# Query factors by way of DRAM, and output tiles spread over three stages of a decoder trunk

## The chip, the cores and the metric

The kernel runs on one core of a Trainium2 chip. The metric is the device time of one execution in microseconds, as the median of several runs. Its engines are named as in the profile: PE (TensorE, with PEld for its weight loads), DVE (VectorE), ACT (ScalarE), POOL (GpSimd) and SP (SyncE, which only issues DMAs here).

## The reference, cut to what matters

One layer of a hybrid decoder, for a prompt of 2048 rows and for 8 samples of 8 rows, 1024 columns, all in float32:

```
x  = x + concat([ha, cb]) @ w_out                  # mLSTM and convolution, output projection
hc = rmsnorm(x, norm_x)
sc = (hc @ x_wq) . mem_k  * M**-0.5                # 4 heads, 256 memory tokens
x  = x + (softmax(sc) . mem_v) @ x_wo              # mem_k, mem_v = rmsnorm(mem) @ x_wk, x_wv
x  = x + (gelu(conv3(fa)) * fg) @ f_wdown          # ConvFFN; y = rmsnorm(x)
```

For the prompt the weights are folded into the memory: since the scores are linear in `hc`, `x_wq . mem_k` is computed once (the key fold) and multiplied with the rows; since the output is linear in the probabilities, `mem_v . x_wo` is computed once too (the value fold). The sample rows have their own memory for each of the 8 samples and are attended without folds (`sample_attention`).

## The kernel before, in words

**Arithmetic.** Every large product is made of three matmuls on float32 numbers split into a high and a low part (`mm3`, L152; `split`, L294: a cast on ACT for the high part, a subtraction on DVE or POOL for the low). The products with the folded weights go by a scheme of seven block products in place of eight; `right_factors` (L1077) turns four blocks of the folded weight into seven factors, `seven_products` uses them, `left_sums` makes the seven left factors of a pair of row tiles.

**Order.** The program names all work in one order; a planner then sets each engine's own order by simulated readiness, with earlier work of the program first. Tiles that share a tag take turns in its buffers, and are given them in the order of the program: tag "xt" of the pool `xtp` has six of 512 KB. Eight PSUM banks are shared too, by turns: banks D and F hold the halves of output tiles, A, G, D and E those of the folds, B and C (and E and F in the key fold) transposes.

**Stages around the change.**

- *Tail* (to about 770 us): end of the mLSTM, convolution tails, and the first eight output tiles. An output tile (`out_part`, L1193) is one of 16 row tiles of 128 rows (a 17th holds the 64 sample rows): `out_load` (L1183) fetches the concatenated rows `craw` and splits them (`ct`), and fetches the rows of x; two halves of 24 matmuls each against `w_out`, one PSUM bank each, are added to x, and the tile is stored to `x1_d`. `TAIL_OUT` says how many are done by here.
- *Memory stage* (`memory_kv`, L1002): 256 memory rows are fetched, normalised and transposed to `hm`, and multiplied with x_wk and x_wv in four halves of 48 matmuls. It is a generator that yields eight times, twice in each half; an output tile follows each second yield.
- *Value fold* (`fold_values`, L1145): `transposed` (L1031) fetches V back from DRAM (`mv`), transposes and splits it to `mT`; the products with x_wo give blocks, and `right_factors` seven factors, stored to DRAM (`mo_d`). It yields ten times; the remaining output tiles lie between. K is transposed here too (`mk`).
- *Key fold* (`fold_keys`, L1091): rows of x_wq are transposed and split (`rows_t`) into the tile `pair`, multiplied with K, scaled, and made into the seven query factors. `put` splits each of the 28 blocks straight into `wf`, which stays in SBUF.
- *Scores* (`scores`, eight pairs of row tiles): `pair_in` (L1399) fetches two row tiles and normalises them, `pair_factors` (L1377) transposes them (banks B, C; copies `a`), sums them on POOL and splits the seven left factors `l`. Seven products, softmax, store.
- *Output rows* (`out_rows`): the value factors are fetched (14 DMAs of 512 KB, tile `raw`, tag "xt") and split into `wf` again; eight pairs of probabilities are handled like the rows before, with the steps of `sample_attention` between, from pair `SIDE_FROM` on, four steps to a pair. After them the ConvFFN begins.

Of the kernel before, what the change touches and what calls it, by code (L numbers as in the profile page):

```python
# [9 lines left out]
F32 = mybir.dt.float32  # L10
# [9 lines left out]
P = 128  # L20
D = 1024
KT = D // P
# [8 lines left out]
N_RAW = 6  # L31

CONV_BLOCKS = [(0, 1, 12), (1, 2, 12), (3, 2, 12), (5, 2, 12), (7, 1, 12)]
TAIL_OUT = 8
MLSTM_STEPS = 2, 1, 1
W2_EARLY = 4
H2_BUFS = 10
# [3 lines left out]
KV_POOL = 2  # L41
OUT_POOL = 10
TAIL_LAG = 8
FV_STEPS = 3
KT_COPY = lambda nc: [nc.vector.tensor_copy] * 2
B_ENG = 2
MO_ENG = lambda nc: [nc.vector, nc.gpsimd, nc.vector, nc.gpsimd]
L_BUFS = 2, 6
FB_BUFS = 6
ROWS_AHEAD = 2  # L50
ROWS_AT = 0
FV_RAW = 4
FV_WT = 6
FT_BUFS = 4
KT_BUFS = 3
SIDE_FROM = 1
NORM_V = 2
L_POOL = ()
A_BUFS = 9
# [36 lines left out]
def trunk_kernel(ctx: ExitStack, tc: tile.TileContext, i: dict, o: list):  # L96
    nc = tc.nc
    V, A, G, T, SY = nc.vector, nc.scalar, nc.gpsimd, nc.tensor, nc.sync
# [8 lines left out]
    def dram(name, shape):  # L107
        return dr.tile(shape, F32, name=name, tag=name)
# [55 lines left out]
    xtp = xw = ctx.enter_context(tc.tile_pool(name="xw", bufs=6, side="right", reuse_waits="tile"))  # L164
# [5 lines left out]
    def banks(*tags):  # L170

        turn = cycle(tags)

        def get():
            tag = next(turn)
            return ps.tile([P, 512], F32, name="ps" + tag, tag=tag, bufs=PS_BANKS[tag])

        return get
# [115 lines left out]
    def split(hi, lo, src, gain=None, eng=None):  # L294
        if gain is None:
            A.copy(hi, src)  # L296
            tt(lo, src, f(hi), ALU.subtract, eng)
        else:
            act(hi, src, AF.Copy, scale=gain)
            stt(lo, src, gain, f(hi), ALU.mult, ALU.subtract)  # L300
# [701 lines left out]
    def memory_kv():  # L1002

        with tc.tile_pool(name="kva", bufs=1, side="right", reuse_waits="tile") as kva:
            xts = []
            for j in range(2):
                t = xtp.tile([P, D], F32, name="xt", tag="xt")
                SY.dma_start(t, i["mem_prompt"][0, j * P:(j + 1) * P, :])
                xts.append((t, P))
            hm = kva.tile([P, 2, KT, M], F32R, name="hm")  # L1010
            norm_x(xts, hm.rearrange("p z k n -> p (z k n)")[:, :D], V)
            make_h(xts, "g_mem", hm, mmps, True)
            for key, out, scr in (("x_wk", memk_p, mk_d), ("x_wv", memv_p, mv_d)):
                for half in range(2):
                    hs = slice(half * 512, half * 512 + 512)
                    pts = [mmps() for _ in range(2)]
                    for k in range(KT):
                        if k % 4 == 0:
                            yield
                        w = load_w(kva, i[key][0][k * P:(k + 1) * P, hs], 512, 3, raws=(kva, 4),  # L1020
                                   eng=G if k % KV_POOL == KV_POOL - 1 else V)[0]
                        for j in range(2):
                            c = slice(j * P, j * P + P)
                            mm3(pts[j], (hm[:, 0, k, c], hm[:, 1, k, c]), (w[:, 0], w[:, 1]), k == 0, k == KT - 1)
                    for j in range(2):
                        t = kva.tile([P, 512], F32, name="kvo", tag="kvo", bufs=2)
                        A.copy(t, pts[j])
                        SY.dma_start(out[0, 0, j * P:(j + 1) * P].rearrange("m h d -> m (h d)")[:, hs], t)
                        SY.dma_start(scr[j][:, hs], t)
# [61 lines left out]
    def fold_keys(pools, mT, ps_, tps_):  # L1091

        def load(j):
            if j < KT:
                raws.append(row_tile(i["x_wq"][0][order[j] * P:(order[j] + 1) * P, :]))

        def rows_t(j):
            load(j + ROWS_AHEAD)
            raw = raws[j]
            wT = pools[j % 2].tile([P, 2, D], F32R, name="pair", tag="pair")  # L1100
            for half in range(2):
                pt = tps_()
                hs = slice(half * 512, half * 512 + 512)
                for k in range(4):
                    transpose(pt[:, k * P:(k + 1) * P], raw[:, half * 512 + k * P:half * 512 + (k + 1) * P])
                split(wT[:, 0, hs], wT[:, 1, hs], pt)
            return wT

        def tmp():
            return pools[1].tile([P, 512], F32, name="ft", tag="ft", bufs=FT_BUFS)  # L1110

        order = [r + z for r in range(KT // 2) for z in (0, KT // 2)]
        raws = []
        for j in range(ROWS_AHEAD):
            load(j)
        yield
        nxt = rows_t(0)
        dst = yield

        def put(q, k, x, eng=None):  # L1120
            split(dst[q][:, 0, k], dst[q][:, 1, k], x, eng=eng)

        bs = []
        for j, r in enumerate(order):
            wT, nxt = nxt, rows_t(j + 1) if j + 1 < KT else None
            for half in range(2):
                pt = ps_()
                for z in range(2):
                    for kt in range(2):
                        k = 4 * half + 2 * z + kt  # L1130
                        c = slice(k * P, k * P + P)
                        mm3(pt[:, z * M:(z + 1) * M], (wT[:, 0, c], wT[:, 1, c]),
                            (mT[:, 0, k], mT[:, 1, k]), kt == 0, kt == 1)
                b = pools[1].tile([P, 512], F32, name="b", tag="b", bufs=FB_BUFS)
                if half < B_ENG:
                    ts(b, pt, col("g_x", r), ALU.mult)
                else:
                    act(b, pt, AF.Copy, scale=col("g_x", r))
                bs.append(b)
            if j % 2:  # L1140
                right_factors(put, r % 4, *bs, tmp, G)
                bs = []
            yield
# [49 lines left out]
    def out_part(t, loaded=None):  # L1193
        nt = P if t < NT else S
        ct, xt = loaded or out_load(t)
        for half in range(2):
            pt = mmps()
            gemm_tm(pt, ct, 0, nt, wout, half)
            hs = slice(half * 512, half * 512 + 512)
            tt(xt[:nt, hs], xt[:nt, hs], pt[:nt], ALU.add)  # L1200
        SY.dma_start(x1_d[t], xt[:nt])

    side = sample_mlstm()
# [84 lines left out]
    outs = list(range(NT))  # L1288
# [64 lines left out]

    tps, smps = banks("B", "C"), banks("E")
    SC = M ** -0.5
    mo_d = [dram(f"mo{q}", [P, KT // 2, 512]) for q in range(7)]
    p_d = [dram(f"p{t}", [P, D]) for t in range(NT)]

    def softmax(pt, p, nt, scale, nscale, w=2):
# [221 lines left out]
    fms = ExitStack()  # L1581
    fm = fms.enter_context(tc.tile_pool(name="fm", bufs=1, reuse_waits="tile"))
    pps = banks("A", "A", "G", "D", "E")
    for j, _ in enumerate(memory_kv()):
        if j % 2:
            out_part(outs.pop(0))
    out_part(NT)
    with tc.tile_pool(name="fv", bufs=1, reuse_waits="tile") as fv:
        out_part(outs.pop(0))
        fold = fold_values(fv, transposed(fv, mv_d, tps), pps,  # L1590
                           lambda: fv.tile([P, 512], F32, name="ft", tag="ft", bufs=FT_BUFS))
        for _ in range(FV_STEPS):
            next(fold, None)
        mT = transposed(fm, mk_d, tps)
        pairs = [fm]
        keys = fold_keys(pairs, mT, pps, banks("E", "F"))
        for j, _ in enumerate(fold):
            if outs:
                out_part(outs.pop(0))
            if j == ROWS_AT:  # L1600
                next(keys)
        while outs:
            out_part(outs.pop(0))
    next(keys)
    wos.close()
    wa2.close()
    wfs = ExitStack()
    wfp = wfs.enter_context(tc.tile_pool(name="wfp", bufs=1, side="right", reuse_waits="tile"))
    fks = ExitStack()
    pairs.append(fks.enter_context(tc.tile_pool(name="fk", bufs=1, side="right", reuse_waits="tile")))  # L1610

    def factors():
        return [wfp.tile([P, 2, KT // 2, 512], F32R, name=f"wf{q}", tag=f"wf{q}") for q in range(7)]

    wf = factors()
    keys.send(wf)
    for _ in keys:
        pass
    xs0 = pair_in(0)
    fms.close()  # L1620
    fks.close()
    aps = ExitStack()
    ap = aps.enter_context(tc.tile_pool(name="ap", bufs=1, reuse_waits="tile"))
    l_turn = cycle([(pa, L_BUFS[0])] * L_BUFS[0] + [(ap, L_BUFS[1])] * L_BUFS[1])
# [5 lines left out]
    pps = banks("A", "A", "G", "D", "F", "E")  # L1630
    nxt = pair_factors(xs0)
    with tc.tile_pool(name="scp", bufs=1, reuse_waits="tile") as scp:
        for p in range(NT // 2):
            left, nxt = nxt, pair_factors(pair_in(p + 1)) if p + 1 < NT // 2 else probs_in(0)
            scores(scp, p, left)
    mo = factors()
    for q in range(7):
        for k in range(0, KT // 2, 2):
            raw = xtp.tile([P, 2, 512], F32, name="raw", tag="xt")
            SY.dma_start(raw, mo_d[q][:, k:k + 2])  # L1640
            for z in range(2):
                split(mo[q][:, 0, k + z], mo[q][:, 1, k + z], raw[:, z], eng=MO_ENG(nc)[k + z])
    pps = banks("A", "A", "G", "D", "F")
    with tc.tile_pool(name="pp", bufs=1, reuse_waits="tile") as pp:
        side = sample_attention(pp)
# [288 lines left out]
```

## Time and profile before

| | us |
|---|---|
| three runs: median (lowest to highest) | 2969.03 (2966.44 to 2973.68) |
| the profiled execution, its own time | 2968.27 |
| its span, first to last instruction | 2966.6 |
| mean granted TensorE clock | 0.972 of full |
| TensorE busy | 2807.9 (95%) |
| DVE, ACT, POOL busy | 2142.2 (72%), 1534.5 (52%), 1109.8 (37%) |

The stages named above stand in the trace at about: tail to 771, memory stage to 875, value fold to 967, key fold to 1024, scores to 1195, output rows to 1450, ConvFFN to the end. A busy engine counts as busy at whatever clock it was granted, so for TensorE the granted clock is read beside its busy time: 1.00 is its upper level, 2.4 GHz, and a matmul takes twice as long at the lower.

### The profile page before, as it was taken

To read this page: it belongs to the slowest core of one execution; us is meant where nothing else is said; L and a number is where in the kernel's file an instruction comes from. 1 tells how busy PE (TensorE), PEld (TensorE's weight loads), DVE (VectorE), ACT (ScalarE), POOL (GpSimd) and SP (SyncE) were. 2 spreads that over 40 slices of the span, in tenths; PEclk is the share of its full clock that TensorE was granted. 3 is DMA by queue.
4 is the path that set the end of the run, shared out by engine and by line. 5 is a ranking of instruction groups with operands and counts; after the bars stand their busy time and mean duration, and the time that the engine had idled before them with its cause. 6 is when DMAs were issued, how large, how long until landed. Compare 5 with 4: busy or idle time off the path is not lost.

```text
span 2966.6 us, 49315 instructions
## 1 busy us (share of the span) xinstructions
PE 2807.9 (95%) x17924; PEld 2479.4 (84%) x17924; DVE 2142.2 (72%) x3937; ACT 1534.5 (52%) x3134; POOL 1109.8 (37%) x1299
## 2 busy tenths in 40 slices
PE   7999989999799799899899999999999999999998
PEld 6889889976678688676588988999989999899987
DVE  4588898873123888744598889878797767877776
ACT  4667678871232765412464446655466545544433
POOL 1558565451120632633433325333253222522222
PEclk9999999997899999999899999999999999999999
DMA  7644433244456423656745555655465545644432
GB/s 185 194 139 160 124 97 117 90 161 152 165 184 222 141 82 109 212 193 240 266 162 169 166 171 195 189 160 160 144 219 160 158 135 162 187 131 133 131 116 76
DMA packets 336939, 471.80 MB, mean 159 GB/s; under 512 B 33421, under 2 KB 238707, under 8 KB 336688
## 3 DMA queue, kind: packets, MB, share of 16 engines
q1 hardware_dynamic: 336696, 468.66, 49.2%
q8 instruction: 141, 2.31, 0.3%
q14 instruction: 102, 0.84, 0.1%
HBM read 361.68 MB, written 107.26 MB: 158 GB/s over the span
## 4 chain that ended last, share of the span: by engine, by line
PE 72%; DVE 14%; DMA 6%; issue 4%; ACT 2%; POOL 1%; SPq 1%; DVEq 0%; POOLq 0%; ACTq 0%
PE psA L150 21%; PE psD L150 14%; PE psF L150 14%; PE psE L150 9%; PE psG L150 9%; DVE psG L124 2%; DMA raw<-in_f_wup 2%; DVE wt L127 2%; PE psC L147 1%; PE psB L147 1%; DVE raw L127 1%; DVE acc L124 1%; DVE u L127 1%; DVE wf L127 1%; DMA xt<-x 1%
## 5 line engine op out<-in xcount | busy, mean ns | idle before, releaser
L296 ACT CAST wt<-raw 128x512 fp32r<-128x512 f32 x872 | 528.8, 620 | 529.2 <-PE psA L150 150.6
L127 DVE TENSOR_TENSOR wt<-raw,wt 128x512 fp32r<-128x512 f32 x660 | 512.2, 792 | 123.5 <-ACT wt L296 119.7
L127 POOL TENSOR_TENSOR wt<-raw,wt 128x512 fp32r<-128x512 f32 x212 | 306.5, 1449 | 703.9 <-ACT wt L296 572.2
L150 PE MATMUL psA<-R,wt 128*128 128x256 f32 (+1 forms) x2448 | 334.1, 287 | 4.1 <-DVE R L124 1.6
L150 PEld LDWEIGHTS psA<-R,wt 128*128 128x128 f32 x2448 | 313.8, 190 | 7.7 <-DVE R L124 1.8
L127 POOL TENSOR_TENSOR cside<-cside,cprod 128x512 f32<-128x512 f32 (+2 forms) x248 | 250.9, 1012 | 123.1 <-ACT cprod L119 90.0
L124 DVE SCALAR_TENSOR_TENSOR psG<-ue,vc,psG 128x512 f32<-128x512 f32 (+2 forms) x448 | 256.9, 573 | 22.8 <-ACT psG L119 16.0
L150 PE MATMUL psA<-wt,ht 128*128 128x512 f32 (+1 forms) x768 | 191.0, 395 | 0.0
L150 PE MATMUL psD<-R,wt 128*128 128x256 f32 (+1 forms) x1248 | 178.5, 288 | 6.7 <-DVE R L127 2.8
L150 PE MATMUL psF<-R,wt 128*128 128x256 f32 (+1 forms) x1248 | 179.3, 288 | 4.4 <-DVE R L124 1.7
L150 PE MATMUL psE<-R,wt 128*128 128x256 f32 (+1 forms) x1224 | 174.3, 287 | 5.8 <-DVE R L127 3.0
L150 PE MATMUL psG<-R,wt 128*128 128x256 f32 (+1 forms) x1224 | 175.3, 288 | 1.9 <-DVE R L124 1.3
L150 PEld LDWEIGHTS psD<-R,wt 128*128 128x128 f32 x1248 | 163.7, 191 | 10.4 <-DVE R L127 3.8
L150 PEld LDWEIGHTS psA<-wt,ht 128*128 128x128 f32 (+1 forms) x768 | 140.6, 185 | 34.9 <-DVE u L127 0.2
L150 PEld LDWEIGHTS psF<-R,wt 128*128 128x128 f32 x1248 | 163.4, 190 | 6.2 <-DVE u L127 2.6
L150 PEld LDWEIGHTS psE<-R,wt 128*128 128x128 f32 x1224 | 159.4, 190 | 9.6 <-DVE R L127 4.3
L150 PEld LDWEIGHTS psG<-R,wt 128*128 128x128 f32 x1224 | 160.3, 191 | 3.1 <-DVE R L124 1.6
L119 ACT ACTIVATE cprod<-ue,vc 128x512 f32<-128x512 f32 (+2 forms) x248 | 146.8, 605 | 28.4 <-POOL cside L127 22.0
L150 PE MATMUL psA<-wf,l 128*128 128x512 f32 x516 | 132.2, 404 | 10.8 <-DVE u L127 5.8
L124 DVE SCALAR_TENSOR_TENSOR y<-fe,vc,y 128x512 f32<-128x512 f32 x176 | 130.5, 778 | 14.4 <-ACT y L119 14.4
L127 POOL TENSOR_TENSOR y<-y,u 128x256 f32<-128x256 f32 x110 | 97.8, 898 | 107.0 <-DVE u L127 89.5
L150 PEld LDWEIGHTS psA<-wf,l 128*128 128x128 f32 x516 | 97.8, 193 | 38.7 <-issue 13.2
(608 smaller groups left out, 6096.1 us busy)
## 6 DMA issues: line engine op xcount, KB each, us to landing
raw<-sum SPq DMA_DIRECT2D x132, 512.0 KB
raw<-in_f_wup SPq DMA_DIRECT2D x110, 512.0 KB
raw<-in_f_wdown SPq DMA_DIRECT2D x88, 512.0 KB
xt<-x SPq DMA_DIRECT2D x48, 512.0 KB
sum<-raw SPq DMA_DIRECT2D x44, 512.0 KB
raw<-in_f_wup SPq DMA_DIRECT2D x66, 256.0 KB
xt<-in_x_prompt SPq DMA_DIRECT2D x32, 512.0 KB
x<-xt SPq DMA_DIRECT2D x32, 512.0 KB
```

The costliest lines, as they stand in the source:

```text
L119: A.activation(out, in_, func, bias=bias, scale=scale)
L124: V.scalar_tensor_tensor(out=out, in0=in0, scalar=s, in1=in1, op0=op0, op1=op1)
L127: (eng or V).tensor_tensor(out=out, in0=a, in1=b, op=op)
L147: T.transpose(out, in_, ident[:n, :n])
L150: T.matmul(out, lhsT, rhs, start=start, stop=stop)
L296: A.copy(hi, src)
```

## The change

Output tiles: six instead of eight are done in the tail. One is loaded ahead of the memory stage and its matmuls are called after the memory stage's first step. Of the other nine, two come between the K/V products, four in the value fold and three in the key fold. The sample's tile (`NT`) stays behind the K/V products.

Query factors: the key fold's `put` stores the 28 blocks to DRAM (`wf_d`, 256 KB each) instead of splitting them; behind the key fold `load_factors` fetches them by 14 DMAs of 512 KB into the tag "xt" and splits them into `wf`, ahead of the first pair's rows. The value factors go through the same function, as before. The key fold's second pool now lies on the left side, where the value fold's was.

Sample attention: its steps lie between the products from pair 0 on instead of pair 1.

```
-TAIL_OUT = 8
+TAIL_OUT = 6
-FV_STEPS = 3
-ROWS_AT = 0
-SIDE_FROM = 1
+SIDE_FROM = 0
@@ fold_keys
         for j in range(ROWS_AHEAD):
             load(j)
-        yield
         nxt = rows_t(0)
-        dst = yield
         def put(q, k, x, eng=None):
-            split(dst[q][:, 0, k], dst[q][:, 1, k], x, eng=eng)
+            SY.dma_start(wf_d[q][:, k], x)
@@ memory stage and folds
-    for j, _ in enumerate(memory_kv()):
-        if j % 2:
+    def next_out(at):
+        if at and outs:
             out_part(outs.pop(0))
+    t = outs.pop(0)
+    loaded = out_load(t)
+    kv = memory_kv()
+    next(kv)
+    out_part(t, loaded)
+    for j, _ in enumerate(kv):
+        next_out(j % 3 == 1)
     out_part(NT)
     with tc.tile_pool(name="fv", bufs=1, reuse_waits="tile") as fv:
-        out_part(outs.pop(0))
         fold = fold_values(fv, transposed(fv, mv_d, tps), pps, ...
-        for _ in range(FV_STEPS):
-            next(fold, None)
         mT = transposed(fm, mk_d, tps)
-        pairs = [fm]
-        keys = fold_keys(pairs, mT, pps, banks("E", "F"))
         for j, _ in enumerate(fold):
-            if outs:
-                out_part(outs.pop(0))
-            if j == ROWS_AT:
-                next(keys)
-        while outs:
-            out_part(outs.pop(0))
-    next(keys)
+            next_out(j % 3 == 0)
+    with tc.tile_pool(name="fk", bufs=1, reuse_waits="tile") as fk:
+        for j, _ in enumerate(fold_keys([fm, fk], mT, pps, banks("E", "F"))):
+            next_out(j % 2 == 0)
+    while outs:
+        out_part(outs.pop(0))
@@ factors
-    wf = factors()
-    keys.send(wf)
-    for _ in keys:
-        pass
+    def load_factors(src):
+        out = factors()
+        for q in range(7):
+            for k in range(0, KT // 2, 2):
+                raw = xtp.tile([P, 2, 512], F32, name="raw", tag="xt")
+                SY.dma_start(raw, src[q][:, k:k + 2])
+                for z in range(2):
+                    split(out[q][:, 0, k + z], out[q][:, 1, k + z], raw[:, z], eng=MO_ENG(nc)[k + z])
+        return out
+    wf = load_factors(wf_d)
     xs0 = pair_in(0)
...
-    mo = factors()
-    for q in range(7):
-...
+    mo = load_factors(mo_d)
```

## Rows read from the trace of the kernel before

**Rows 1.** the page, part 1: busy us (share) xinstructions.

```profile
PE 2807.9 (95%) x17924; PEld 2479.4 (84%) x17924; DVE 2142.2 (72%) x3937; ACT 1534.5 (52%) x3134; POOL 1109.8 (37%) x1299
```

**Rows 2.** stretches: PE, PEld, DVE, ACT, POOL busy us; PEclk, DMA, GB/s.

```profile
745.80:790.90 45.10, 29.84 (x138) 22.87 (x137) 10.25 (x21) 12.35 (x20) 9.02 (x5) 0.80 0.47 167
...
874.70:966.60 91.90, 91.59 (x420) 73.34 (x421) 33.54 (x49) 25.68 (x44) 0.00 (x0) 1.00 0.66 226
966.60:1023.70 57.10, 40.12 (x286) 37.32 (x286) 48.35 (x63) 41.10 (x74) 35.51 (x36) 0.91 0.51 166
1023.70:1050.50 26.80, 22.18 (x94) 17.33 (x93) 25.86 (x28) 16.58 (x30) 17.72 (x15) 0.94 0.09 30
...
1195.50:1250.00 54.50, 43.62 (x193) 35.20 (x193) 37.59 (x57) 26.01 (x60) 31.69 (x29) 0.91 0.66 212
```

**Rows 3.** timeline of the DMA-issue queue: start us, us, what is issued.

```profile
771.85 0.36 SPq L1008 DMA_DIRECT2D xt<-in_mem_prompt  x1
...
842.82 0.33 SPq L1190 DMA_DIRECT2D xt<-in_x_prompt  x1
...
877.70 1.72 SPq L1036 DMA_DIRECT2D xt<-mv  x2
...
889.98 0.33 SPq L1036 DMA_DIRECT2D xt<-mk  x1
```

**Rows 4.** timeline of PE in the value fold: start us, us, tile.

```profile
909.02 4.55 PE L150 MATMUL psF<-wt,ct 128*128 128x512 f32 x19
...
919.97 0.61 PE L150 MATMUL psD<-wt,mT 128*128 128x512 f32 x2
...
928.57 2.89 PE L150 MATMUL psD<-wt,ct 128*128 128x512 f32 x12
```

**Rows 5.** timeline of PE, from the tail into the memory stage.

```profile
781.88 0.48 PE L147 MATMUL psD<-ident,xt 128*128 128x128 f32 x1 [10.72 <-ACT xt L119]
...
790.91 4.21 PE L150 MATMUL psD<-wt,hm 128*128 128x512 f32 x9 [0.66 <-DVE hm L124]
...
805.40 5.75 PE L150 MATMUL psD<-wt,ct 128*128 128x512 f32 x24 [0.22 <-ACT kvo L1027]
810.99 5.60 PE L150 MATMUL psF<-wt,ct 128*128 128x512 f32 x24
```

**Rows 6.** the table of stretches, for the start of the ConvFFN.

```profile
1447.70:1475.00 27.30, 15.65 (x64) 12.12 (x62) 24.71 (x37) 16.83 (x36) 15.08 (x16) 0.64 0.98 332
```

**Rows 7.** tile wf: duration ns min/median/max, first and last start us, forms.

```profile
L296 ACT CAST wf<-raw x28: 612/622/630, 1179.4 to 1212.0; 128x512 fp32r<-128x512 f32 x28
...
L127 DVE TENSOR_TENSOR wf<-raw,wf x14: 678/1190/1782, 1180.1 to 1216.3; 128x512 fp32r<-128x512 f32 x14
L127 POOL TENSOR_TENSOR wf<-raw,wf x14: 1292/1696/1742, 1180.6 to 1213.3; 128x512 fp32r<-128x512 f32 x14
```

**Rows 8.** tiles xt and a, in the same form.

```profile
L121 ACT ACTIVATE junk<-xt x35: 1042/1057/1068, 983.4 to 2526.8; 128x1024 bf16<-128x1024 f32 x33, 32x1024 bf16<-32x1024 f32 x2
...
L296 ACT CAST l<-a x112: 602/619/666, 993.9 to 1417.3; 128x512 fp32r<-128x512 f32 x112
L127 DVE TENSOR_TENSOR l<-a,l x112: 670/686/1803, 996.8 to 1419.6; 128x512 fp32r<-128x512 f32 x112
L127 POOL TENSOR_TENSOR a<-a x64: 1267/1296/1808, 1000.6 to 1413.9; 128x512 f32<-128x512 f32 x64
L1386 ACT COPY a<-psB x32: 567/586/603, 992.4 to 1409.3; 128x512 f32<-128x512 f32 x32
```

**Rows 9.** timelines of PE and GpSimd, ends of the output rows.

```profile
1201.35 5.34 PE L150 MATMUL psA<-wf,l 128*128 128x512 f32 x12 [5.83 <-DVE u L127]
...
1237.03 7.34 PE L150 MATMUL psA<-wf,l 128*128 128x512 f32 x24 [4.00 <-ACT l L296]
...
1452.39 0.69 PE L147 MATMUL psB<-ident,xt 128*128 128x128 f32 x2 [4.08 <-ACT b L119]
...
1436.13 1.27 POOL L127 TENSOR_TENSOR xt<-xt,u 128x512 f32<-128x512 f32 x1 [12.21 <-DMA xt<-x]
```

More of the change, by code (lines that the diff above doesn't have):

```diff
@@ L1355, in trunk_kernel @@
     SC = M ** -0.5
-    mo_d = [dram(f"mo{q}", [P, KT // 2, 512]) for q in range(7)]
+    mo_d, wf_d = [[dram(f"{x}{q}", [P, KT // 2, 512]) for q in range(7)] for x in ("mo", "wfd")]
     p_d = [dram(f"p{t}", [P, D]) for t in range(NT)]
@@ L1608, in trunk_kernel @@
     wfp = wfs.enter_context(tc.tile_pool(name="wfp", bufs=1, side="right", reuse_waits="tile"))
-    fks = ExitStack()
-    pairs.append(fks.enter_context(tc.tile_pool(name="fk", bufs=1, side="right", reuse_waits="tile")))
     def factors():
         return [wfp.tile([P, 2, KT // 2, 512], F32R, name=f"wf{q}", tag=f"wf{q}") for q in range(7)]
-    wf = factors()
-    keys.send(wf)
-    for _ in keys:
-        pass
+    def load_factors(src):
[8 more added lines that the diff above has]
+    wf = load_factors(wf_d)
     xs0 = pair_in(0)
     fms.close()
-    fks.close()
     aps = ExitStack()
@@ L1635, in trunk_kernel @@
             scores(scp, p, left)
-    mo = factors()
-    for q in range(7):
[L1638 to L1642, printed above, removed]
+    mo = load_factors(mo_d)
     pps = banks("A", "A", "G", "D", "F")
```

## The prediction

> **What bounds the kernel now.** I read the page first: TensorE (PE) is busy for 95% of the span [rows 1], so time can come only from stretches in which it is idle or granted less than full clock. Then a table of stretches around the change [rows 2]. The reader is to see that the value fold (874.7 to 966.6) has no idle left (91.59 of 91.90 us at clock 1.00), while the key fold (966.6 to 1023.7) has 17.0 us idle at clock 0.91 with VectorE (DVE) busy 48 of 57, the first score pair 4.6 us, the step from tail to memory stage 15.3 us at clock 0.80, and the first output rows 10.9 us. The change moves output tiles from the full stretches to the key fold. Last, timelines, for the order in which buffers are given out, since that decides what the new reload waits for.
>
> **A rule of this kernel that the trace shows.** Buffers of one tag are handed out in program order, even when a later user is ready first. SBUF: after the load at 842.82 no load into the six "xt" buffers is issued until 877.70 [rows 3], although output tiles ended in between (at 839 and 863, going by the sequence of tiles of 11 us) and gave two buffers back, and the mk rows had long been written; mv is ahead in the program, and its last block is only then in DRAM. mk follows at 889.98. PSUM: the output tile's half in bank F runs at 909.02, its half in bank D only at 928.57, after the fold's own use of D at 919.97 [rows 4], though the operands are the same. I let this rule decide the new order.
>
> **The change part by part.** An output tile is 48 matmuls. A half of 24 starts 5.59 us after the other [rows 5], so a tile is 11.0 us wherever PE is the limit. No arithmetic is added; every term below is idle time gained or lost.
>
> *Tail and memory stage: +3, and +1.* Two tiles (22 us) leave the tail. One is loaded ahead and called behind the memory rows' transposes. The old gap: the memory rows' load is issued at 771.85 [rows 3], PE stands still for 10.72 us up to the first transpose at 781.88, the first product is at 790.91, and this runs 9 matmuls in 4.2 us, half speed [rows 5]. The forwarded tile cannot fill the gap: the eight transposes use banks D and F and come first in the program, and so the tile starts where the products started. Its two loads go ahead of the memory rows' (1 MB, some 3 us at 332 GB/s [rows 6]). The half-speed stretch is then the tile's instead of the product's. I take +3. Ends: -8, if the tail's last small work slips between the matmuls of its last tile and the rows are fetched earlier, and +6, two loads later and the norm's small steps behind the tile's split. Two of the four halves of the K/V products now follow one another directly, so that bank D is waited for: +1 (0 to 2).
>
> *Value fold: +3.* The cover between the last K/V product and the first fold product is now one tile (the sample's, 11 us), where there were three and a half. The reload of mv is issued about 3 us after that product (877.70 against 874.7); load, transposes and splits took 33 us behind other tiles, but their own steps sum to some 9 (estimate: 4 for the load, as for the memory rows, and 5 for transposes and splits). So 12 against a cover of 11; +3 for the loads of weights beside it. Ends 0 and +8. Afterwards four tiles (44 us) cover the fold as before.
>
> *Key fold: -21.* Three tiles (33 us) come in, and 28 splits (ScalarE cast and DVE or GpSimd subtraction) go to a later place. With all idle covered, the stretch takes 33 us and the old work, 40.1 us busy at clock 0.91, that is 36.5 at full: 69.5 in place of 57.1 + 33 = 90.1. DVE has 48.4 us now, less 16 subtractions; it is no limit in 69. So -21. What could spoil it: bank F is shared by row transposes and tiles in program order, and so the rows wait behind each tile; the other end is -8. The added 28 DMA stores (256 KB each, 7.3 MB) pass the same queue as the row loads: over 69 us that is 106 GB/s beside the 166 of before, below the 332 that rows 6 show.
>
> *Reload of the query factors: +25.* It takes the place of the direct splits. There are 14 loads of 512 KB, each with two casts and two subtractions, in the order factor by factor, k pairs within. The second load already reads the last k row, which is stored only at the end of the key fold. By the rule, it holds back the other twelve, and behind these pair 0's two row loads, which stood ahead of everything before. Count from the last key matmul: the first wait ends at about 2 us (a store, by the mv reload, takes about as long); the other loads are 11 x 0.524 MB and then one row tile, 6.3 MB at 332 GB/s [rows 6] = 19 us, with 2 to land: pair 0's first row is there at about 24. GpSimd keeps pace: 14 subtractions of 1.70 = 24 us [rows 7]. Then square 1.06, two small steps, scale, transpose, copy 0.59, cast 0.62, subtraction 0.69 [rows 8], with the hops some 6 to 7 us: the first product at 31. The third product needs the sum chain, four GpSimd additions of 1.30 [rows 8], a cast and a subtraction after the second row tile: about 38 to 39. Five products of 12 matmuls follow, 2.7 us each: the pair ends at about 52. Before, from 1023.7 to 1050.5, it was 26.8 [rows 2]. So +25. Low end: factors and rows stream without the wait, which leaves +3. High end: the pace of the other reload, whose 28 casts went from 1179.4 to 1212.0 [rows 7], with the last subtraction at 1216: 37 us to the rows in place of 24, so +38.
>
> For the transfers alone a page would say less. Rows 6 have 332 GB/s at a DMA share of 0.98. The Trainium skill, "DMA: Bandwidth & Descriptors", section "Anatomy of one DMA — SWDGE (gpsimd) path", fits about 2 us plus the bytes at 436 GB/s, for another issuing engine; 6.3 MB would then be 16.4 us instead of 21, and this sum some 5 us lower. I keep the measured rate.
>
> The 28 splits are neither saved nor added; only their engines change, from 16 DVE and 12 GpSimd to 14 and 14.
>
> *Sample attention from pair 0: -6.* At the start of the output rows PE waits 5.83 and 4.00 us, and at the end of the stage 4.08 [rows 9]. The side work starts and ends a pair earlier. It may fill some of the first two, and lets the rows of the next stage be normalised before the last pair ends. Against it: its nine loads go ahead of pair 1's rows in the buffer queue. GpSimd then stands as it does now at the end (12.21 us for a row load [rows 9]) and holds pair 2's sums. In between PE is full, so nothing is to be had there. I take -6, of the 14 that could go; ends -12 and +6.
>
> **Sum.** 3 + 1 + 3 - 21 + 25 - 6 = +5. The profiled execution took 2968.27 us (span 2966.6 and 1.7 around it), 0.8 below the median of 2969.03. 2968.3 + 5 = 2973. No difference is what a measurement calls anything within 0.3%, 9 us: 2960 to 2978.
>
> **Rivals.**
> - *The reload hides (faster).* If pair 0's rows are fetched ahead of the held-back factors and the factors arrive as they are stored, the reload costs +3: 2951. For it: first pairs' rows were fetched during the key fold until now, and factor B11 is complete some 4 us before the last key matmul. Against it: mk behind mv in rows 3.
> - *The reload goes at the pace of the other one (slower).* Reload +38, side work 0 because its loads meet those of the second reload: 3 + 1 + 3 - 21 + 38 + 0 = +24, 2992. It decides from the point where more than 35 us pass between last key matmul and first score product. For it: rows 7. Against it: there the buffers of the old factors had to come free as well, here they are free.
> - *The tiles don't mesh with the key rows.* Bank F makes rows and tiles alternate: key fold -8 instead of -21, with all else as forecast: +18, 2986. For it: rows 4, a half held for 19 us by the order of one bank. Against: each tile is called with one row already transposed, so that PE has its products.
>
> **Chances.** Forecast 0.36, reload hidden 0.29, slow reload 0.23, no meshing 0.12. The likeliest gives 2973, with its own range 2962 to 2982; the tails of the forecast fall about evenly to both sides. Faster 0.30, within 0.3% 0.35, slower 0.35. The range takes in the first rival and most of the other two: 2948 to 2995.
>
> **What would show it.** In the profile after: the loads of the raw factors, all but the first, issued behind the last key matmul, and pair 0's row loads behind them; PE idle for some 25 to 30 us there, then half clock; the key-fold stretch at clock 1.00 and some 70 us long with three tiles in it; the forwarded tile starting only after the last memory transpose; the first wait of the output rows shorter. I am wrong where the row loads are issued before the last raw factors, where key rows wait in ScalarE's casts while bank F holds a tile, or where other stretches (tail up to 745, the scores after pair 1, the ConvFFN after 1475) move by more than 3 us, since I hold them unchanged.

## The result and the profile after

The changed kernel takes 2990.02 us (median of 7 runs, 2977.93 to 2995.07), the kernel before 2968.28 (7 runs, 2962.64 to 2973.68): a ratio of 1.0073, 95% interval 1.0053 to 1.0094. It is slower, inside the range (2948 to 2995), and outside the forecast's own range of 2962 to 2982; the price is that of the rival "slow reload" (2992).

The page of the changed kernel, span and part 1, beside [rows 1]:

```profile
span 2993.4 us, 49433 instructions
...
PE 2814.6 (94%) x17924; PEld 2488.5 (83%) x17924; DVE 2137.2 (71%) x3935; ACT 1537.2 (51%) x3134; POOL 1102.2 (37%) x1301
```

Busy TensorE time is nearly the same; the span is 26.8 us longer. Not all of that belongs to the change. Up to the same product in the tail (its start is called the tail's point: 727.63 before, 735.22 after) every engine has the same instructions, 4810 matmuls among them. The table of stretches, of the kernel before and then of the changed one (columns as in [rows 2]):

```profile
0.00:727.63 727.63, 663.46 (x4810) 613.47 (x4810) 531.45 (x1141) 473.64 (x1164) 362.22 (x483) 0.96 0.46 140
```

```profile
0.00:735.22 735.22, 669.83 (x4810) 619.70 (x4810) 530.60 (x1141) 474.15 (x1164) 362.15 (x483) 0.95 0.45 139
```

The same instructions took 7.6 us more in the profiled execution of the changed kernel, with the granted clock at 0.95 in place of 0.96. So all further times are counted from points that both programs have:

| from ... to ... | before, us | after, us | after - before |
|---|---|---|---|
| the tail's point (727.63; 735.22) to the last key matmul (1023.80; 1006.41) | 296.2 | 271.2 | -25.0 |
| to the first output product (1201.35; 1222.99) | 177.6 | 216.6 | +39.0 |
| to the first twelve matmuls in a row into bank G in the ConvFFN (1494.70; 1519.58) | 293.4 | 296.6 | +3.2 |
| to the end of the span | 1471.9 | 1473.8 | +1.9 |

Two of these points stand in no row so far, the last key matmuls and the twelve into bank G of the kernel before:

```profile
1022.44 1.36 PE L150 MATMUL psA<-mT,pair 128*128 128x256 f32 x10
...
1494.70 1.58 PE L150 MATMUL psG<-R,wt 128*128 128x256 f32 x12
```

The changed part is the first three lines, +17.3, where the forecast had +5. The stretches of the changed kernel that answer to [rows 2]: from tail to memory stage, start of the value fold, value fold, key fold, reload, first pair:

```profile
756.60:777.30 20.70, 4.73 (x17) 2.34 (x16) 5.44 (x12) 11.43 (x19) 6.66 (x4) 0.58 0.86 307
...
859.40:874.10 14.70, 12.10 (x56) 7.27 (x56) 1.84 (x3) 1.54 (x4) 0.00 (x0) 1.00 0.89 315
874.10:942.70 68.60, 68.47 (x313) 56.50 (x314) 35.94 (x51) 26.25 (x43) 2.41 (x1) 1.00 0.79 281
942.70:1006.40 63.70, 63.52 (x401) 56.74 (x399) 32.58 (x47) 12.41 (x20) 10.35 (x8) 1.00 0.58 200
1006.40:1038.10 31.70, 0.03 (x2) 0.03 (x1) 19.98 (x17) 18.24 (x32) 23.30 (x17) 0.55 0.96 343
1038.10:1071.20 33.10, 28.48 (x117) 22.70 (x118) 16.64 (x26) 26.79 (x47) 18.06 (x25) 0.82 0.29 91
```

The key fold runs at clock 1.00 with 63.52 of 63.70 us busy. In the 31.7 us behind it (1006.40 to 1038.10) PE does nothing and the clock is at 0.55; in the next stretch it is at 0.82, so part of the first pair too runs at the lower level of 1.2 GHz.

Why PE is idle there is seen in three timelines. SP's queue (start, us, what is issued):

```profile
862.11 1.78 SPq L1034 DMA_DIRECT2D xt<-mv  x2
863.94 0.90 SPq L1034 DMA_DIRECT2D xt<-mk  x2
...
981.54 0.38 SPq L1616 DMA_DIRECT2D raw<-wfd  x1
...
1005.21 0.32 SPq L1616 DMA_DIRECT2D raw<-wfd  x1
...
1006.20 0.38 SPq L1616 DMA_DIRECT2D raw<-wfd  x1
...
1015.70 10.92 SPq L1616 DMA_DIRECT2D raw<-wfd  x6
1027.97 23.09 SPq L1400 DMA_DIRECT2D xt<-x  x10
```

The second factor load goes out at 1005.21, 24 us after the first; the other twelve follow; pair 0's row loads come only behind them, at 1027.97 (ten loads in a row, the next pairs' among them). At 862.11 and 863.94 stand mv and mk, which were 12 us apart in [rows 3]. PE then, from the last key matmuls on:

```profile
1003.61 2.80 PE L148 MATMUL psA<-mT,pair 128*128 128x256 f32 x22
1038.08 1.12 PE L145 MATMUL psB<-ident,xt 128*128 128x128 f32 x4 [31.67 <-DVE xt L129]
...
1041.42 1.22 PE L148 MATMUL psA<-wf,l 128*128 128x512 f32 x2 [0.44 <-ACT l L294]
...
1054.80 1.22 PE L148 MATMUL psG<-wf,l 128*128 128x512 f32 x2 [4.08 <-ACT l L294]
...
1071.20 0.60 PE L145 MATMUL psB<-ident,xt 128*128 128x128 f32 x4
```

PE waits 31.67 us for the first row; the first product starts at 1041.42, the third at 1054.80. GpSimd's and ScalarE's timelines say what the row waited for:

```profile
1019.99 16.34 POOL L125 TENSOR_TENSOR wf<-raw,wf 128x512 fp32r<-128x512 f32 x10 [0.66 <-ACT wf L294]
1036.41 0.19 POOL L131 TENSOR_SCALAR v<-ss 128x1 f32<-128x1 f32 x1
1036.68 0.55 POOL L141 TENSOR_TENSOR r<-v,nhalf 128x1 f32<-128x1 f32 x1
```

```profile
1032.68 1.06 ACT L119 ACTIVATE junk<-xt 128x1024 bf16<-128x1024 f32 x1 [0.15 <-DMA xt<-x]
1033.64 0.18 ACT L119 ACTIVATION_READ_ACCUMULATOR junk<-xt 128x1 f32 x1
```

The row's square is summed by 1033.8, but the two small steps to its inverse root stand behind ten subtractions of the reload, which end at 1036.3.

### The profile page after: what moved, and what is told of

The parts are those of the page before. It is cut to its first block, busy times and chain, and to the rows that moved or that the text cites. A ratio compares the mean times of both kernels' runs of the same rounds, so it can differ in the third digit from the quotient of the medians.

```text
span 2993.4 us, 49433 instructions
## 1 busy us (share of the span) xinstructions
PE 2814.6 (94%) x17924; PEld 2488.5 (83%) x17924; DVE 2137.2 (71%) x3935; ACT 1537.2 (51%) x3134; POOL 1102.2 (37%) x1301
## 4 chain that ended last, share of the span: by engine, by line
PE 74%; DVE 11%; DMA 8%; issue 3%; ACT 2%; POOL 1%; SPq 1%; DVEq 0%; POOLq 0%; ACTq 0%
PE psA L148 22%; PE psD L148 15%; PE psF L148 15%; PE psE L148 10%; PE psG L148 9%; DMA raw<-in_f_wup 2%; DVE wt L125 2%; DVE psG L122 2%; PE psB L145 1%; PE psC L145 1%; DVE raw L125 1%; DVE acc L122 1%; DMA h<-h 1%; DVE u L125 1%; DMA xt<-x 1%
```

## The experiments

Ratios are to the kernel before, with their 95% intervals; the changed kernel has 1.0073. The stretch from the last key matmul to the first output product, 177.6 us before and 216.6 after, is called the reload stretch.

**The detour alone.** To the kernel before, the stores and the reload are added; tiles and sample attention stay.

```
-            split(dst[q][:, 0, k], dst[q][:, 1, k], x, eng=eng)
+            SY.dma_start(wf_d[q][:, k], x)
...
+    for q in range(7):
+        for k in range(0, KT // 2, 2):
+            raw = xtp.tile([P, 2, 512], F32, name="raw", tag="xt")
+            SY.dma_start(raw, wf_d[q][:, k:k + 2])
...
     xs0 = pair_in(0)
```

> The kernel before with one part of the change: the key fold stores its factors to DRAM, and they are fetched and split ahead of the first pair's rows; output tiles and sample attention stay as before. Theory that the parts add up: the reload costs the 38 us that it costs in the changed kernel, and the key fold without the 28 splits gets some 10 of its 17 idle us back: 2968 + 28 = 2996. Rival, that the reload is dear only because the spread tiles keep the key fold and its transfers late: half of the price, 2978.

Measured 1.0058 (1.0039 to 1.0076). The key fold and the reload in its table of stretches:

```profile
965.29:1003.20 37.91, 32.40 (x253) 31.13 (x251) 28.82 (x45) 11.31 (x20) 9.35 (x8) 0.95 0.81 278
1003.20:1038.00 34.80, 0.00 (x0) 0.00 (x0) 22.56 (x18) 18.25 (x32) 24.28 (x18) 0.54 0.94 311
```

From its first product (965.29) the key fold takes 37.9 us without any tile in it, 5.5 of them idle, where [rows 2] has 57.1 and 17.0; 32 transposes of the first two pairs' rows, which [rows 2] has in that stretch, now lie behind it. The reload stretch is 217.1, as in the changed kernel. So both large terms come from the detour: its key fold ends 21.4 us earlier (274.7 us from the tail's point in place of 296.2), and its reload costs 39.6. The expected sum of parts was 11 too high, since the fold gained 21 and not 10.

**Two tiles back in the tail.**

```
-TAIL_OUT = 6
+TAIL_OUT = 8
```

> The changed kernel with TAIL_OUT back at 8: two tiles return to the tail, and one is left in the key fold in place of three. By the prediction's reason for the key fold's -21 (tiles cover its idle time) two thirds of that are lost: 2986 + 14 = 3000, less 3 for the step to the memory stage. Rival: it was the 28 splits that made the key fold idle. With the splits gone and no tile in it, its stretch took 36.6 us with 5.5 idle in the run wfd_only, where it had 57.1 with 17.0 idle before; then two tiles less cost at most 4: 2986 to 2990.

Measured 1.0082 (1.0068 to 1.0096), 2.7 us above the changed kernel by the ratios, and their intervals overlap. Tiles in the key fold are worth a few us, not two thirds of 21. The rival holds.

**Sample attention from pair 1 again.**

```
-SIDE_FROM = 0
+SIDE_FROM = 1
```

> The changed kernel with SIDE_FROM back at 1: the sample attention's steps lie between the products from pair 1 on. By the prediction's term (-6 for starting at pair 0) this run is 6 slower than the changed kernel: 1.0073 x 2964.6 = 2986, so 2992. Rival, from the traces: the wait at the first output product is 5.83 before and 5.82 after, and the ConvFFN's first steady product is no nearer to the start of the output rows; then starting a pair earlier is worth nothing: 2986.

Measured 1.0058 (1.0043 to 1.0073): 4 us below the changed kernel, less than the two intervals can part, and not 6 above. From first output product to the ConvFFN's bank G it is 293.0 us (1217.91 to 1510.86), with 293.4 before and 296.6 in the changed kernel. Over all thirteen profiles of this document this stretch is 292.0 to 296.6 in the seven kernels that start at pair 0 and 290.7 to 293.4 in the six that start at pair 1. The changed kernel's lines:

```profile
1222.99 5.18 PE L148 MATMUL psA<-wf,l 128*128 128x512 f32 x12 [5.82 <-DVE u L125]
...
1455.06 0.74 PE L148 MATMUL psA<-wf,l 128*128 128x512 f32 x2 [3.28 <-ACT l L294]
...
1471.74 0.44 PE L145 MATMUL psB<-ident,xt 128*128 128x128 f32 x2 [1.08 <-ACT b L117]
...
1476.79 2.93 PE L148 MATMUL psA<-R,wt 128*128 128x256 f32 x12 [2.66 <-DVE R L125]
...
1519.58 1.58 PE L148 MATMUL psG<-R,wt 128*128 128x256 f32 x12
```

The first wait is 5.82, as in [rows 9]. The 4.00 us there and the 4.08 at the end of the stage are gone or smaller (1.08), but 3.28 has come in at the last pair and 2.66 in the ConvFFN's first products. Starting a pair earlier moved waits and saved none. This kernel also differs from the detour alone only by the spread of the tiles (and, with it, the place of the key fold's pool and of its first row loads). Both have 1.0058, with intervals of about 5 us to each side. From the tail's point to the end of the span its profile is 6.3 us shorter (2251.9 and 2258.2), 4.1 of them up to the last key matmul.

**Pair 0's rows ahead of the factors.**

```
-    wf = load_factors(wf_d)
     xs0 = pair_in(0)
+    wf = load_factors(wf_d)
```

> The changed kernel with one edit: pair 0's two rows are fetched and normalised in the program ahead of the reload of the query factors. In the changed kernel 64.8 us pass from the last key matmul (1006.4) to the end of pair 0's products (1071.2), where the kernel before took 26.8. Order theory: most of that is pair 0's rows standing behind fourteen factor loads, and their normalisation behind GpSimd's subtractions; with the rows ahead, the transposes run beside the key fold, the first score product comes within 15 us of the last key matmul in place of 35, the products follow the factors as they come, and the pair ends some 40 us after the last key matmul; less some 5 us for pair 1's rows, which are then late: 2990 - 20 = 2970. Volume theory: 7.3 MB and 28 splits after the last key matmul are the price in whatever order; only the four small steps of the rows are saved, 4 us: 2986.

Measured 1.0009 (0.9998 to 1.002), 19 us below the changed kernel. SP's queue and PE:

```profile
973.63 0.38 SPq L1400 DMA_DIRECT2D xt<-x  x1
...
975.33 0.32 SPq L1400 DMA_DIRECT2D xt<-x  x1
...
979.65 0.32 SPq L1616 DMA_DIRECT2D raw<-wfd  x1
...
998.08 0.79 SPq L1616 DMA_DIRECT2D raw<-wfd  x2
```

```profile
1001.66 1.88 PE L148 MATMUL psA<-wf,l 128*128 128x512 f32 x7
...
1020.74 1.22 PE L148 MATMUL psG<-wf,l 128*128 128x512 f32 x2 [7.15 <-ACT l L294]
...
1043.37 1.12 PE L145 MATMUL psB<-ident,xt 128*128 128x128 f32 x4 [5.35 <-ACT a L1382]
```

GpSimd's and ScalarE's timelines, for what these two waits end with:

```profile
996.42 5.59 POOL L125 TENSOR_TENSOR a<-a 128x512 f32<-128x512 f32 x4
...
1016.48 3.69 ACT L294 CAST wf<-raw 128x512 fp32r<-128x512 f32 x6 [1.41 <-DMA raw<-wfd]
1020.07 2.70 ACT L294 CAST l<-a 128x512 fp32r<-128x512 f32 x5
...
1042.75 0.56 ACT L1382 COPY a<-psB 128x512 f32<-128x512 f32 x1
```

The rows are fetched at 973.63 and 975.33, and the first score product follows the last key matmul (1001.82) at once. The reload stretch is 198.5 in place of 216.6. What is left: 7.15 us for the third product and 5.35 for pair 1's second row. The third product's four sums end on GpSimd at 1002.0, but ScalarE casts them only from 1020.07 on, behind twelve casts of the reload (1009.69 to 1020.2) that wait for their loads; and the transposes of the second row wait until ScalarE has copied the first row out of bank B, at 1042.75, behind squares and scalings of later rows. So it is ScalarE's order that holds both, not GpSimd. The order theory is right; the volume is the same and the price half: 20.9 us over the 177.6 of the kernel before, where it was 39.0.

**The k pairs outside.**

```
-        for q in range(7):
-            for k in range(0, KT // 2, 2):
+        for q, k in order:
...
-    wf = load_factors(wf_d)
+    wf = load_factors(wf_d, [(q, k) for k in (0, 2) for q in range(7)])
```

> The changed kernel with one edit: the factors are fetched with the pairs of k rows outside and the seven factors inside, so that the first seven loads read what the key fold has stored 20 us before its end. Order theory: the second load, which reads the last k row, held back the other twelve; now six loads (as many as there are buffers) are issued ahead of the last key matmul, some 3 MB or 9 us less lie behind it, and pair 0's rows come 9 to 12 us earlier: 2980. Volume theory: the loads were held by the buffers or by the place of the factors, not by the last k row: no difference, 2990.

Measured 1.0046 (1.003 to 1.0063), 8 us below the changed kernel, by intervals that overlap; the reload stretch is 209.1 us in place of 216.6. Loads two to seven are issued before the last key matmul (999.58); of SP's queue the second load, the sixth and seventh, and the rows:

```profile
971.83 0.32 SPq L1615 DMA_DIRECT2D raw<-wfd  x1
...
989.36 1.14 SPq L1615 DMA_DIRECT2D raw<-wfd  x2
...
1014.06 25.72 SPq L1400 DMA_DIRECT2D xt<-x  x10
```

Ten row loads begin 14.5 us behind the last key matmul (1014.06), where it was 21.6. So the last k row did hold the other loads back, for 7 us of the 9 to 12 expected.

**GpSimd taken out of the reload.**

```
-                    split(out[q][:, 0, k + z], out[q][:, 1, k + z], raw[:, z], eng=MO_ENG(nc)[k + z])
+                    split(out[q][:, 0, k + z], out[q][:, 1, k + z], raw[:, z], eng=engs[k + z])
...
-    wf = load_factors(wf_d)
+    wf = load_factors(wf_d, [V] * 4)
```

> The changed kernel with one edit: all 28 subtractions of the reload of the query factors go to VectorE, none to GpSimd. In the changed kernel GpSimd's last subtraction ends at 1036.3 and the first row's inverse root waits for it, although the row's sum of squares was there at 1033.8. If GpSimd's pace sets the start of the scores, first transposes come 3 to 4 us earlier: 2985 to 2987. If the transfers set it, no difference: 2990 (VectorE then has 28 x 0.69 = 19 us of work in the 26 us of the loads).

Measured 1.0063 (1.0047 to 1.008), 3 us below, which the intervals alone would not part. The mechanism shows in GpSimd's and DVE's timelines:

```profile
1034.54 0.19 POOL L131 TENSOR_SCALAR v<-ss 128x1 f32<-128x1 f32 x1 [18.90 <-ACT junk L119]
...
1026.27 7.70 DVE L125 TENSOR_TENSOR wf<-raw,wf 128x512 fp32r<-128x512 f32 x12 [0.84 <-ACT wf L294]
```

GpSimd has been idle for 18.90 us when the sum arrives, and PE's wait is 28.30 in place of 31.67; the reload stretch is 211.5 us in place of 216.6.

**Both orders together, and with GpSimd free.** The edits of the two order runs; in the second kernel VectorE as well.

```
-    wf = load_factors(wf_d)
     xs0 = pair_in(0)
+    wf = load_factors(wf_d, [(q, k) for k in (0, 2) for q in range(7)])
...
+    wf = load_factors(wf_d, [(q, k) for k in (0, 2) for q in range(7)], [V] * 4)
```

> The changed kernel with both edits, pair 0's rows ahead of the reload and the pairs of k rows outside. If both waits (rows behind factors, factors behind the last k row) are priced apart, the gains of 19 (rows_first) and 8 (k_outer) add: 2986 - 27 = 2959. Rival: with the rows ahead the limit is no longer the factors but the left sums on GpSimd (7.15 us before the third product in the run rows_first) and pair 1's rows (5.35 us): then no better than rows_first, 2967.

> As rows_k, with all 28 subtractions of this reload on VectorE. If the left sums wait on GpSimd behind the reload's subtractions, the third product's wait (7.15 us in rows_first) falls to under 2 and the time is 5 to 6 below rows_k: 2954. Rival: VectorE, which also makes the left factors' low parts, becomes the limit: same as rows_k or slower.

Measured 1.002 (1.0007 to 1.0033) and 1.0001 (0.9991 to 1.0011). The prices don't add: with the rows ahead, k outside is worth nothing, since the first product now needs the eighth load. PE in the first of the two:

```profile
1000.70 3.01 PE L148 MATMUL psA<-wf,l 128*128 128x512 f32 x12 [2.28 <-DVE b L129]
1009.91 0.79 PE L148 MATMUL psA<-wf,l 128*128 128x512 f32 x1 [6.20 <-ACT wf L294]
```

With GpSimd free the ratio is 5.6 us lower, the expected size, and the third product starts 18.8 us behind the last key matmul in place of 23.4. But the wait that the expectation names, 7.15 us, was 1.95 already in the first of the two, so its reason is not shown.

**Rows, VectorE and SIDE_FROM 1, factor by factor.**

```
-SIDE_FROM = 0
+SIDE_FROM = 1
...
-    wf = load_factors(wf_d)
     xs0 = pair_in(0)
+    wf = load_factors(wf_d, [V] * 4)
```

> The changed kernel with three edits: pair 0's rows ahead of the reload, the reload's subtractions on VectorE, sample attention from pair 1. The factors are fetched factor by factor again, because in the run rows_k the first product waited 6.20 us for its second half of k, which came eighth. If the three prices are apart (rows -19, GpSimd -3 to -6, sample attention -4), 0.994 to 0.997 of the kernel before in place of 1.0073: 2950 to 2956. Rival: the price is now set by pair 0's chain, whatever these do: as rows_first, 1.0009, 2967.

Measured 1.0000 (0.9988 to 1.0012): nearer to the rival than to the sum of the single gains. These add up to 26 us and the run has 22; as each of them is known to some 7 us only, the difference by itself doesn't show that they overlap.

**Pair 1's rows ahead of the last four factors**, on top of that.

```
+            if q == ahead:
+                ready[1] = pair_in(1)
             for k in range(0, KT // 2, 2):
...
+    wf = load_factors(wf_d, [V] * 4, 3)
```

> As rows_dve_side1, with pair 1's rows fetched and normalised in the program ahead of the last four factors. If the waits behind pair 0's products (5.35 us in rows_first) come from pair 1's rows standing behind the factor loads, 4 to 6 us less than rows_dve_side1. Rival: the row buffers that they hold and the steps that they add to ScalarE delay the factors by as much: no difference.

Measured 0.9970 (0.9956 to 0.9983), median 2955.79 us against 2964.6 for the kernel before, 9 us below. The reload stretch is 189.9 us, 4.6 less than without this edit, as expected. It beats both kernels.

**The detour, rows ahead, tiles where they were**, against the detour alone.

```
+    xs0 = pair_in(0)
     for q in range(7):
...
-                split(wf[q][:, 0, k + z], wf[q][:, 1, k + z], raw[:, z], eng=MO_ENG(nc)[k + z])
+                split(wf[q][:, 0, k + z], wf[q][:, 1, k + z], raw[:, z], eng=V)
-    xs0 = pair_in(0)
```

> The kernel before with the detour of the factors through DRAM alone, pair 0's rows ahead of the reload and its subtractions on VectorE; output tiles where they were. Theory that the spread of the tiles is worth nothing (side1 and wfd_only, which differ by the spread alone, both had 1.0058): same as rows_dve_side1. Rival: the spread tiles hide part of the reload once the rows are ahead, since they keep PE busy while the first factors come: 5 to 8 us slower than rows_dve_side1.

Measured 1.0045 (1.0027 to 1.0064), 13 us above its counterpart with spread tiles. The key folds of the two, first this kernel, then the counterpart:

```profile
963.79:1010.80 47.01, 36.98 (x269) 34.44 (x267) 33.12 (x50) 16.25 (x30) 14.67 (x15) 0.93 0.73 246
```

```profile
944.88:1006.30 61.42, 59.89 (x391) 54.06 (x389) 34.89 (x50) 17.13 (x29) 14.99 (x14) 1.00 0.66 224
```

With the norm and transposes of pair 0's rows in it, the key fold without tiles is 47.0 us, 10.0 of them idle at clock 0.93; with three tiles it is 61.4, 1.5 idle, at 1.00. From the tail's point to the end of the span the two profiles are 6.5 us apart (2245.3 and 2238.8), as much as the 6.3 us of the pair without the rows ahead. So the spread is worth about 6 us by the traces in both; that it is worth more once the rows are there, as the ratios would have it (0 and 13 us), is not shown.

## Where the forecast was right and where it was wrong, step by step

The likeliest value, 2973, was 17 us too low. That 2990 lies in the range of 2948 to 2995 is owed to the width that the rivals gave it, and in part to luck: the trace has the price of the slow reload without its reason, and a fold term 6 us better than forecast beside it.

- *Tail and memory stage, +4.* The forwarded tile starts behind the last transpose, as said:

```profile
768.62 0.47 PE L145 MATMUL psD<-ident,xt 128*128 128x128 f32 x1 [12.01 <-ACT xt L117]
...
777.32 7.25 PE L148 MATMUL psD<-wt,ct 128*128 128x512 f32 x24 [0.66 <-DVE hm L122]
...
874.13 0.74 PE L148 MATMUL psA<-wt,mT 128*128 128x512 f32 x2 [2.63 <-ACT mT L294]
```

  The gap before the transposes is 12.01 us (10.72 in [rows 5]). From the tail's point to the tile behind the last K/V product (874.90; 859.37) it was 147.3 us before and 124.2 after, with two tiles (22.0) less: -1.1. Inside the ends of -8 and +8.
- *Value fold, +3.* The reload of V takes 12 us (862.11 to 874.13) against one tile: 2.6 us idle. Right.
- *Key fold, -21.* Near in size, wrong in reason. From there to the last key matmul it is 148.9 before and 147.0 after, with two tiles more: -23.9 (both fold terms together, -18 forecast). The detour alone ends the key fold 21.4 us earlier without moving a tile. I had counted the splits as moved but the idle time as filled by tiles. Not all of the 21.4 is idle time that the splits made: with pair 0's rows back in the key fold (the last run: 282.9 us from the tail's point to the last key matmul) 13.2 are left, and about 8 are rows' work that only moved behind the fold. The forecast's old work of 40.1 us still held the 32 transposes of these rows. What tiles alone would fill, with the splits in place, no run shows. The rival "no meshing" did not occur: 63.52 of 63.70 us busy.
- *Reload, +25.* This term decided, and it was mis-sized. From last key matmul to the end of pair 0 it was 64.8 us (1006.41 to 1071.20) where 26.8 had been: +38. The order of the queue was as forecast, and the row came at 26 us (24 forecast). Three things were wrong or missing. The sum counted 11 loads where 13 were left, the second to the fourteenth: with the row that is 7.3 MB, 22 us at 332 GB/s, which with the forecast's 2 us before and 2 behind gives the 26. "GpSimd keeps pace" took no account of when the splits could start: they ended 30 us after the last key matmul, and the row's inverse root waited 2.6 us behind them on the same engine; so the first product came at 35.0 and not at 31. And behind it the pair took 30 us, not 21: the first products ran in part at half clock (0.82 granted in the stretch), and the next pairs' rows, whose loads arrive together with pair 0's, had their first steps between pair 0's: pair 1's 16 transposes on PE, six squares on ScalarE (1.06 us each, between 1039.7 and 1051.6) and small steps on GpSimd between the four sums. The third product came at 48.4 instead of 38 to 39.
  The stretch moved 343 GB/s at a DMA share of 0.96, near the 332 of [rows 6]. The 436 GB/s that the Trainium skill ("DMA: Bandwidth & Descriptors", section "Anatomy of one DMA — SWDGE (gpsimd) path") fits for another issuing engine were not reached on this queue, and the measurement decides.
- *Sample attention, -6.* Nothing was gained: +3.2 by the traces of the two kernels, and -4 when it is undone, which the intervals alone would not part. The first wait of the output rows, which was to shrink, is 5.82.
- *The sum.* -1.12 - 23.86 + 39.03 + 3.24 = +17.29. The slow reload had the right price (+38), and the first product stood at its bound of 35 us behind the last key matmul, but not for its reason: the raw rows came at 26 us, not at the 37 of the value factors' pace.

The medians stand 21.7 us apart. That the reload's order is the larger part is shown by moving the rows (-19). How the rest of its price divides between clock, sums and the next pairs' rows was not tried singly. Of the stretches that the forecast held unchanged, the scores from the end of pair 0 to the first output product moved by 0.9 us (150.9 to 151.8) and the ConvFFN by 1.9. The tail moved by 7.6, more than the 3 that was to be a sign of error; the last section says why this cannot be told from the spread between executions.

## What to carry to other kernels

When work is sent by way of DRAM, look at what is queued behind it: with the rows ahead the detour came out even here (1.0009), and with the rows behind fourteen loads and ten subtractions its reload cost twice as much. Before a gap is covered with other work, look at what its engine waits for: the key fold ended 21.4 us earlier with no tile in it, and the spread of the tiles was worth about 6 more by the traces. Count work that only moves to the next stretch there, not as a gain. Gains of edits on one chain need not add: -19 and -8 gave -16 together, since the second edit put a load that the first product needs into eighth place.

## What the runs showed that was not expected

Identical work took 721.5 to 737.6 us in thirteen profiles, from the start to the same product in the tail. That is as much as most terms of this sum, so two traces are compared from a common point. The granted clock over that stretch was 0.95 or 0.96 in all thirteen.

With the rows ahead, the next wait is in ScalarE's order: the third product's sums are ready at 1002.0 and their casts start at 1020.07, behind casts that wait for loads (with VectorE and SIDE_FROM 1, at 1006.5 and 1019.81). No run moved these casts.
